# Accumulating over six visits: the running sum of a column tile kept in PSUM by two ScalarE copies instead of one VectorE addition

## The chip, the cores and the metric

The kernel runs on one core of a Trainium2 chip. The metric is device time in microseconds (us), from several executions; the kernel before takes 1729.73 us, the median of three runs between 1729.15 and 1729.89 us. Engines are named as in the profile: PE is TensorE (PEld its weight loads), DVE is VectorE, ACT is ScalarE, SP issues the DMAs.

## What is computed

One layer of a convolutional decoder block on 256 tokens of width 4096, all in float32:

```
mod = silu(c) @ w_ada + b_ada ; shift, scale, gate = split(mod)
h   = rmsnorm(x) * norm_g * (1 + scale) + shift
P   = h @ w_in                      # 4096 x 14336: a_b a_c a_x a_z (mixer A), b_v b_g b_z (mixer B), 2048 columns each
y_A = a_b * conv3(a_c * a_x) * silu(a_z)
y_B = silu(layernorm(conv31(b_v * sigmoid(b_g)) + bias)) * silu(b_z)
x   = x + gate * ([y_A, y_B] @ w_out)
out = rmsnorm(x) * final_g
```

## The kernel before

**Products.** The 4096 rows of the contraction are 32 contraction tiles of 128, the 14336 columns of the input projection are 28 column tiles of 512 (each 2 token tiles x 512 columns, 1024 numbers in each of 128 partitions). A weight load holds two contraction tiles of one column tile (512 KB) and is one step. For each step ScalarE rounds the raw weights `w_r` to `w_h` (L143), VectorE takes the rest `w_l` (L144), and TensorE runs 12 products (L156 to L158: three products for each of two contraction tiles and two token tiles). The weights of the next step are split ahead (`AHEAD = 1`), and there are three buffers for each of `w_h` and `w_l`, so the split of a step can start when the products three steps before it are done. The input projection has 448 steps and the output projection 128.

**Visits.** The activations `hT` of a contraction tile exist only when the conditioning (`mod_steps`, L174, and `make_h`) has reached it. So the contraction is cut into six blocks, and each column tile is visited once per block: 163 visits of 1 to 7 steps (where one block ends with the tile that the next begins with, the two are one visit). The visits in the stretch that is here called the single-step stretch (start of the second block) have one step each; those of the blocks after it have two or three, those of the last block four. Each visit gets a PSUM tile `ps` from the pool `pmm` (three buffers of two banks). At the end of a tile's first visit ScalarE copies `ps` into the SBUF tile `acc[e]` (L467, 28 times); at the end of every other visit VectorE adds `ps` to `acc[e]` (L469, 135 times). These instructions are written right behind the products of the visit.

**Last block.** When a column tile has had its last visit its epilogue follows: tiles 20 to 23 start `glu_B` (a sigmoid, L352, a VectorE product, transposes on TensorE, copies L360 and the first tap L364 on ScalarE) and then 30 taps of the width-31 convolution, spread over the steps (`conv_tap`: four ScalarE products L370 into `pr`, one VectorE addition L371); tiles 12 to 15 start `silu_gate_A` (L324 to L341); tiles 24 to 27 get a silu in place (L480). The taps run on into the output projection. Beside this, the gate columns are worked out from the last block on: the first 2048 on TensorE (L231), whose PSUM tile `gateps` holds one of the three `pmm` buffers meanwhile, the others on VectorE in the output projection.

**Order.** Each engine works through its own queue in a fixed order. `next_w` loads and splits the weights of the next step and then runs the background work that is due at this step (`run_due`); the products of the step follow.

Of the kernel before, what the change touches and what calls it, by code (L numbers as in the profile page):

```python
# [17 lines left out]
P = 128  # L18
D = 4096            # model width
S = 256             # tokens  # L20
NS = S // P         # token tiles
KT = D // P         # contraction tiles
CT = 512            # columns of one product tile
NE = 7 * 2048 // CT  # column tiles of the input projection
NDT = D // CT       # column tiles of the output projection
NB = 16             # channel tiles of mixer B
# [3 lines left out]
BLOCKS = (4, 4, 4, 6, 6, 8)  # contraction tiles done together; the conditioning of a block is  # L30
                             # worked out while the products of the blocks before run
EARLY = {0: 12, 1: 10}  # column tiles, the first of a block, that stop KD contraction tiles short of it
KD = 2              # contraction tiles of one weight load, which is a step
AHEAD = 1           # steps that weights are split ahead
LEAD = 2            # steps from the conditioning of contraction tiles to their first products
KEEP = 3            # chunks of x.T that stay from the row statistics
HOLD = 5            # steps of the last column tile whose weights stay on chip for the second token tile
GATE_PE = (0, 1)    # gate columns (1024 each) worked out on TensorE, the others on VectorE
GATE_RUN = {0: (0, 70), 1: (70, 115), 2: (115, 185), 3: (185, 231)}  # when, in steps from the last block on
A_SPAN = 5          # steps over which the epilogue of 512 channels of mixer A runs  # L40
# steps of the output projection
CONV_END = 43       # when the convolution of mixer B ends
NORM_AT = 45        # when its layernorm starts
NORM_SPAN = 20      # over which it runs
LOAD_AT = 1         # when the residual of a column tile is loaded
TILE_SPAN = 4       # over which a column tile is finished

# columns of the packed small parameters
# [10 lines left out]
def _segments():  # L59
    """[block, column tile, from, to contraction tile] of the input projection, in the order of the products"""  # L60
    order = [16, 20, 17, 21, 18, 22, 19, 23]
    order += [e + i for i in range(4) for e in (4, 8, 0, 12)]
    order += [24, 25, 26, 27]
    segs, done = [], dict.fromkeys(order, 0)
    for b in range(len(BLOCKS)):
        for n, e in enumerate(order if (len(BLOCKS) - 1 - b) % 2 == 0 else order[::-1]):
            k0, k1 = done[e], sum(BLOCKS[:b + 1]) - (KD if n < EARLY.get(b, 0) else 0)
            done[e] = k1
            if n == 0 and b:
                segs[-1][0], segs[-1][3] = b, k1  # L70
            else:
                segs.append([b, e, k0, k1])
    return segs
# [3 lines left out]
FIRST_USE = {}      # contraction tile: the step that needs it first  # L77
for _t, _k in enumerate(k for _, _, k0, k1 in SEGS for k in range(k0, k1, KD)):
    FIRST_USE.setdefault(_k, _t)
UNITS = [[0, KD]]   # contraction tiles conditioned together: the first, their number  # L80
# [8 lines left out]
def decoder_block(ctx: ExitStack, tc: tile.TileContext, x, c, w_mod, w_gate, w_in, w_out, xt, pk, b_gate, final_g, out):  # L89
# [18 lines left out]
    # ---------------- constants and small parameters  # L108
# [17 lines left out]
    def rsqrt(y, v, t):  # L126
        """y = v ** -0.5; v is kept, t is scratch."""
        nc.scalar.activation(out=t, in_=v, func=AF.Sqrt)
        nc.vector.reciprocal(out=y, in_=t)
        nc.vector.tensor_tensor(out=t, in0=y, in1=y, op=ALU.mult)  # L130
        nc.vector.tensor_tensor(out=t, in0=t, in1=v, op=ALU.mult)
        nc.vector.tensor_scalar(out=t, in0=t, scalar1=-0.5, scalar2=1.5, op0=ALU.mult, op1=ALU.add)
        nc.vector.tensor_tensor(out=y, in0=y, in1=t, op=ALU.mult)

    # ---------------- products: out[s, c] += a[k, s] * w[k, c], each operand as two 12-bit parts
# [10 lines left out]

    def products(ps, act, parts, k0, first, last, tokens=range(NS)):
        """act[k // 2][:, k % 2, hi/lo, s] is stationary; ps [P, NS, CT]."""
        hi, lo = parts
        for i in range(KD):  # L150
            a = act[(k0 + i) // 2]
            f, l = first and i == 0, last and i == KD - 1
            for s in tokens:
                out = ps[s] if isinstance(ps, list) else ps[:, s]
                ah, al = (a[:, (k0 + i) % 2, h, s * P:(s + 1) * P] for h in range(2))
                nc.tensor.matmul(out, ah, hi[:, i], start=f, stop=False)  # L156
                nc.tensor.matmul(out, ah, lo[:, i], start=False, stop=False)  # L157
                nc.tensor.matmul(out, al, hi[:, i], start=False, stop=l)  # L158

    def split_act(dst, src):  # L160
        """dst [P, 2, hi/lo, S] <- src [P, 2, S]"""
        nc.scalar.copy(dst[:, :, 0], src)  # L162
        nc.vector.tensor_tensor(out=dst[:, :, 1], in0=src, in1=dst[:, :, 0].bitcast(F32), op=ALU.subtract)

    # ---------------- conditioning: silu(c) @ w_ada, 1024 columns at a time
# [10 lines left out]
    def mod_steps(k0, n):  # L176
        """Shift and scale of contraction tiles k0 .. k0 + n."""
        state = {}

        m = 4 // n      # contraction rows per load  # L180
# [26 lines left out]
    def gate_steps(ci):  # L207
        """Gate of columns 1024 ci .. 1024 ci + 1024, in all partitions."""
# [14 lines left out]
        def step_t(j):  # L223
            # four products with one stationary column each run side by side in the array
            if j == 0:
                state["ps"] = pmm.tile([P, NS, CT], F32, tag="ps", name=f"gateps{ci}")
            raws_ = [load(j), load(j + 1)]
            for i in range(2):
                for h in range(2):
                    r = 32 * (2 * i + h)  # L230
                    nc.tensor.matmul(state["ps"][r:r + 1, 0], cact[:, j + i:j + i + 1], raws_[i][:, h * CT:(h + 1) * CT], start=j == 0, stop=j == KT - 2)  # L231
# [23 lines left out]
    def make_h(k0, n):  # L255
        """h.T = (x * rstd * norm_g * (1 + scale) + shift).T of contraction tiles k0 .. k0 + n, split"""
# [14 lines left out]
    # ---------------- start: row statistics of x, conditioning of the first block  # L271
    kept = []           # x.T of the first contraction tiles

    def x_stats():
        """1 / rms of the rows of x, in all partitions"""
# [28 lines left out]
    # ---------------- background work, spread over the product steps  # L304
    queue = []          # (step at which it is due, closure)
# [9 lines left out]
    # ---------------- mixer epilogues  # L315
    yT = {}

    def silu_gate_A(i, acc):
        """y_A.T of channels [512 i, 512 i + 512), in pieces"""
# [53 lines left out]
    def mean_B(src, name):  # L373
        """mean over the channels: tiles on VectorE, partitions on TensorE"""
# [10 lines left out]
    def norm_B():  # L385
        """layernorm over the channels (partitions), silu, in pieces"""
# [35 lines left out]
    # ---------------- input projection, by blocks of the contraction  # L422
# [8 lines left out]
    def next_w():  # L431
        """the weights of this step; those of the next steps are loaded and split ahead of other work"""
# [7 lines left out]
    # the conditioning runs evenly beside the products  # L440
    hull = [(0, KD)]    # (step, contraction tiles done by then)
# [17 lines left out]
    for b, e, k0, k1 in SEGS:  # L459
        ps = pmm.tile([P, NS, CT], F32, tag="ps", name=f"ps{k0}_{e}")  # L460
        for k in range(k0, k1, KD):
            parts = next_w()
            step += 1
            products(ps, hT, parts, k, k == k0, k + KD == k1)
        if k0 == 0:
            acc[e] = bigt(f"acc{e}")
            nc.scalar.copy(acc[e], ps)  # L467
        else:
            nc.vector.tensor_tensor(out=acc[e], in0=ps, in1=acc[e], op=ALU.add)  # L469
        if k1 < KT:  # L470
            continue
# [6 lines left out]
        elif e >= 24:  # L478
            zB[e - 24] = acc[e]
            nc.scalar.activation(out=acc[e], in_=acc[e], func=AF.Silu)  # L480
        elif 12 <= e < 16:
            work = silu_gate_A(e - 12, acc)
            spread(work, step, step + A_SPAN)

    # ---------------- output projection: the channels of mixer A, then those of mixer B
# [5 lines left out]
    for dt in range(NDT):  # L491
        ps = pmm.tile([P, NS, CT], F32, tag="ps", name=f"pa{dt}")
        for k in range(0, KT // 2, KD):
            parts = next_w()
            step += 1
            products(ps, yT, parts, k, k == 0, k + KD == KT // 2)
# [3 lines left out]
    # gate, residual, final norm  # L500
# [4 lines left out]
    def finish_tile(dt, ps):  # L505
        """gate, residual, sums of squares and final weight of a column tile, in pieces"""
# [60 lines left out]
    # the last column tile: the first token tile's products, then the second's while the first is finished  # L567
# [28 lines left out]
def _columns(a):  # L596
    """[n * 128, ...] -> [128, n, ...], flat per partition"""
# [35 lines left out]
```

## Time and profile before

| | |
|---|---|
| median of three runs | 1729.73 us |
| span of the profiled execution | 1728.9 us |
| what lies around the span, against the median | 0.8 us |
| PE busy | 1669.5 us, 97% |
| DVE busy | 1506.9 us, 87% |
| ACT busy | 937.0 us, 54% |
| DMA | 302 GB/s in the mean |

The table's shares are means over the whole span; the work differs by stage. The input projection's second block begins near 177 us, its last block runs from about 984 to 1354 us, and the output projection follows. A PE that is 97% busy has its matmuls overlapping one another (each lasts some 390 ns and the next starts after 227 ns), so its delays are seen better in the distance between steps than in its busy share: twelve products at full pace take 2.72 us.

### The profile page before, as it was taken

The page shows a single profiled execution, that of the slowest core. Times are in us where ns is not written, and L with a number is a line of the kernel's source. Part 1 is how long each engine was busy: PE and PEld are TensorE (multiplying, and loading weights), DVE is VectorE, ACT ScalarE, POOL GpSimd, SP SyncE. Part 2 cuts the span into 40 slices and gives each one's busy share as a digit, 9 for nine tenths or more (in the row PEclk, how much of TensorE's full clock was granted, in tenths as well). Part 3 has the DMA queues.
Part 4 walks back from the last instruction along what each step waited for, and adds up shares of the span by engine and source line. Part 5 has one row for each costly group of instructions (what it writes and reads, how often), then busy time and mean ns, then how long its engine had stood idle before and what let it go on. Part 6 is the DMA issues. An engine that isn't in the chain of part 4 may idle for free.

```text
span 1728.9 us, 21319 instructions
## 1 busy us (share of the span) xinstructions
PE 1669.5 (97%) x7480; PEld 1340.1 (78%) x7480; DVE 1506.9 (87%) x1490; ACT 937.0 (54%) x1304; POOL 2.9 (0%) x10
## 2 busy tenths in 40 slices
PE   2899999999999999999999999999999999999997
PEld 1778788888888888888888877777777887878885
DVE  7887998899898988898898857898998999989996
ACT  3555443443334333343333468888887888564443
POOL 0000000000000000000000000000000000000000
PEclk8899999999999999999999999999999999999998
DMA  9899899999999998999899977766888888779993
GB/s 387 327 317 331 300 344 327 325 320 332 310 335 326 330 326 302 312 352 329 292 340 321 327 243 248 253 230 232 288 278 281 277 286 280 266 254 335 361 345 116
DMA packets 145715, 522.42 MB, mean 302 GB/s; under 512 B 16196, under 2 KB 16196, under 8 KB 145608
## 3 DMA queue, kind: packets, MB, share of 16 engines
q1 hardware_dynamic: 145464, 520.71, 85.8%
q8 instruction: 58, 0.95, 0.2%
q10 hardware_dynamic: 144, 0.35, 0.1%
q14 instruction: 49, 0.40, 0.1%
HBM read 516.81 MB, written 4.19 MB: 301 GB/s over the span
## 4 chain that ended last, share of the span: by engine, by line
PE 86%; DVE 6%; DMA 4%; issue 3%; ACT 1%; SPq 0%; DVEq 0%; ACTq 0%
PE ps L156 23%; PE ps L157 23%; PE ps L158 23%; PE pb L158 3%; PE pb L156 3%; PE pb L157 3%; DVE w_l L144 2%; PE gateps L231 2%; DMA gate<-in_w_gate 2%; DVE cv L371 1%; PE pa L157 1%; PE pa L158 1%; DVE modacc L174 1%; PE pa L156 1%; DMA mod<-in_w_mod 1%
## 5 line engine op out<-in xcount | busy, mean ns | idle before, releaser
L143 ACT CAST w_h<-w_r 128x1024 fp32r<-128x1024 f32 x576 | 603.7, 1052 | 654.2 <-PE ps L158 490.4
L144 DVE TENSOR_TENSOR w_l<-w_r,w_h 128x1024 fp32r<-128x1024 f32 x576 | 700.8, 1220 | 118.8 <-ACT w_h L143 113.2
L156 PE MATMUL ps<-w_h,hT 128*128 128x512 f32 x1792 | 705.8, 394 | 3.0 <-ACT hT L162 2.6
L157 PE MATMUL ps<-w_l,hT 128*128 128x512 f32 x1792 | 700.7, 391 | 5.6 <-DVE w_l L144 5.6
L158 PE MATMUL ps<-w_h,hT 128*128 128x512 f32 x1792 | 699.4, 390 | 0.0
L156 PEld LDWEIGHTS ps<-w_h,hT 128*128 128x128 f32 x1792 | 337.5, 188 | 96.8 <-issue 10.8
L157 PEld LDWEIGHTS ps<-w_l,hT 128*128 128x128 f32 x1792 | 337.5, 188 | 79.9 <-DVE w_l L144 10.9
L158 PEld LDWEIGHTS ps<-w_h,hT 128*128 128x128 f32 x1792 | 337.3, 188 | 70.6
L174 DVE SCALAR_TENSOR_TENSOR modacc<-mod,cact,modacc 128x512 f32<-128x512 f32 (+1 forms) x341 | 337.4, 990 | 4.6 <-DMA mod<-in_w_mod 1.5
L370 ACT ACTIVATE pr<-uT,pks 128x255 f32<-128x255 f32 (+14 forms) x480 | 198.1, 487 | 2.1 <-DVE cv L371 1.6
L469 DVE TENSOR_TENSOR acc<-ps,acc 128x1024 f32<-128x1024 f32 x135 | 164.9, 1221 | 22.9 <-PE ps L158 22.4
L371 DVE TENSOR_TENSOR cv<-cv,pr 128x1020 f32<-128x1020 f32 (+14 forms) x120 | 138.7, 1156 | 27.1 <-ACT pr L370 26.4
L157 PE MATMUL pa<-w_l,yT 128*128 128x512 f32 x256 | 100.6, 393 | 2.4 <-DVE w_l L144 2.4
L156 PE MATMUL pa<-w_h,yT 128*128 128x512 f32 x256 | 100.1, 391 | 0.0
L156 PE MATMUL pb<-w_h,yT 128*128 128x512 f32 x256 | 100.1, 391 | 0.0
L158 PE MATMUL pb<-w_h,yT 128*128 128x512 f32 x256 | 100.0, 391 | 0.0
L158 PE MATMUL pa<-w_h,yT 128*128 128x512 f32 x256 | 100.0, 390 | 0.0
L157 PE MATMUL pb<-w_l,yT 128*128 128x512 f32 x256 | 99.6, 389 | 0.0
L174 DVE SCALAR_TENSOR_TENSOR gateacc<-gate,cact,gateacc 128x1024 f32<-128x1024 f32 x62 | 79.4, 1280 | 5.8 <-DMA gate<-in_w_gate 5.6
L157 PEld LDWEIGHTS pa<-w_l,yT 128*128 128x128 f32 x256 | 48.0, 188 | 14.6 <-DVE w_l L144 4.8
L467 ACT COPY acc<-ps 128x1024 f32<-128x1024 f32 x28 | 28.5, 1017 | 51.7 <-PE ps L158 51.7
L156 PEld LDWEIGHTS pb<-w_h,yT 128*128 128x128 f32 x256 | 48.1, 188 | 10.3 <-ACT w_h L143 0.2
(129 smaller groups left out, 645.2 us busy)
## 6 DMA issues: line engine op xcount, KB each, us to landing
w_r<-in_w_in SPq DMA_DIRECT2D x448, 512.0 KB, 5.2
mod<-in_w_mod SPq DMA_DIRECT2D x256, 512.0 KB, 5.1
gate<-in_w_gate SPq DMA_DIRECT2D x128, 512.0 KB, 4.8
w_r<-in_w_out SPq DMA_DIRECT2D x128, 512.0 KB, 5.1
xs<-in_xt SPq DMA_DIRECT2D x8, 512.0 KB, 10.2
xr<-in_x SPq DMA_DIRECT2D x8, 512.0 KB, 7.0
out<-o SPq DMA_DIRECT2D x16, 256.0 KB, 2.7
xc<-in_xt SPq DMA_DIRECT2D x4, 512.0 KB, 5.2
```

Of the source, the lines that this page charges most:

```text
L143: nc.scalar.copy(hi, raw)
L144: nc.vector.tensor_tensor(out=lo, in0=raw, in1=hi.bitcast(F32), op=ALU.subtract)
L156: nc.tensor.matmul(out, ah, hi[:, i], start=f, stop=False)
L157: nc.tensor.matmul(out, ah, lo[:, i], start=False, stop=False)
L158: nc.tensor.matmul(out, al, hi[:, i], start=False, stop=l)
L174: nc.vector.scalar_tensor_tensor(out=acc, in0=raw, scalar=cact[:, j:j + 1], in1=acc, op0=ALU.mult, op1=ALU.add)
L231: nc.tensor.matmul(state["ps"][r:r + 1, 0], cact[:, j + i:j + i + 1], raws_[i][:, h * CT:(h + 1) * CT], start=j == 0, stop=j == KT - 2)
L370: nc.scalar.activation(out=pr[:, j, sh:], in_=u[:, j, :S - sh], func=AF.Copy, scale=cbw[:, 4 * i + j, TAPS - 1 - sh:TAPS - sh])
L371: nc.vector.tensor_tensor(out=o[:, :, sh:], in0=o[:, :, sh:], in1=pr[:, :, sh:], op=ALU.add)
L467: nc.scalar.copy(acc[e], ps)
L469: nc.vector.tensor_tensor(out=acc[e], in0=ps, in1=acc[e], op=ALU.add)
```

## The change

The sum of a column tile is now held in PSUM during a visit. Ahead of a visit that is not the tile's first, ScalarE copies `acc[e]` into the visit's `ps` (`seed`), written at the last step of the visit before; the products of the visit then add to it (`start` is set only where the contraction starts at tile 0). At the end ScalarE copies `ps` back to `acc[e]` (`take`), and for the last visit of tiles 24 to 27 this copy is the silu itself, in place of the silu on `acc[e]`. `take`, with the epilogue that it starts, is written one step later than before: in the first step of the next visit, behind that step's weight split and background work. There is no VectorE addition. Elsewhere only comments and docstrings went.

```
-    def products(ps, act, parts, k0, first, last, tokens=range(NS)):
+    def products(ps, act, parts, k0, first, last, tokens=range(NS), seeded=False):
...
-                nc.tensor.matmul(out, ah, hi[:, i], start=f, stop=False)
+                nc.tensor.matmul(out, ah, hi[:, i], start=f, stop=False, skip_group_check=seeded)
...
-    for b, e, k0, k1 in SEGS:
+    pending = []
+    def seed(n):
+        _, e, k0, _ = SEGS[n]
         ps = pmm.tile([P, NS, CT], F32, tag="ps", name=f"ps{k0}_{e}")
-        for k in range(k0, k1, KD):
-            parts = next_w()
-            step += 1
-            products(ps, hT, parts, k, k == k0, k + KD == k1)
-        if k0 == 0:
+        if k0:
+            nc.scalar.copy(ps, acc[e])
+        return ps
+    def take(e, k1, ps):
+        nonlocal conv_start
+        if e not in acc:
             acc[e] = bigt(f"acc{e}")
-            nc.scalar.copy(acc[e], ps)
-        else:
-            nc.vector.tensor_tensor(out=acc[e], in0=ps, in1=acc[e], op=ALU.add)
+        nc.scalar.activation(out=acc[e], in_=ps, func=AF.Silu if k1 == KT and e >= 24 else AF.Copy)
         if k1 < KT:
-            continue
+            return
         if 20 <= e < 24:
...
         elif e >= 24:
             zB[e - 24] = acc[e]
-            nc.scalar.activation(out=acc[e], in_=acc[e], func=AF.Silu)
         elif 12 <= e < 16:
...
+    ps = seed(0)
+    for n, (b, e, k0, k1) in enumerate(SEGS):
+        for k in range(k0, k1, KD):
+            parts = next_w()
+            step += 1
+            while pending:
+                pending.pop()()
+            if k + KD == k1 and n + 1 < len(SEGS):
+                ps_next = seed(n + 1)
+            products(ps, hT, parts, k, k == 0, k + KD == k1, seeded=k0 > 0)
+        pending.append(lambda e=e, k1=k1, ps=ps: take(e, k1, ps))
+        ps = ps_next
...
+            while pending:          # in the first half of the output projection
+                pending.pop()()
             products(ps, yT, parts, k, k == 0, k + KD == KT // 2)
```

## Rows read from the trace of the kernel before

**Rows 1.** The page: busy time, share of the span and instructions of each engine.
```profile
PE 1669.5 (97%) x7480; PEld 1340.1 (78%) x7480; DVE 1506.9 (87%) x1490; ACT 937.0 (54%) x1304; POOL 2.9 (0%) x10
```
**Rows 2.** The page: busy tenths in 40 slices of 43 us.
```profile
PE   2899999999999999999999999999999999999997
...
DVE  7887998899898988898898857898998999989996
ACT  3555443443334333343333468888887888564443
```
**Rows 3.** The page: the chain that ended last, by engine.
```profile
PE 86%; DVE 6%; DMA 4%; issue 3%; ACT 1%; SPq 0%; DVEq 0%; ACTq 0%
```
**Rows 4.** Waits of PE, 80 to 1560 us (us in total, times, longest).
```profile
PE ps L157 <- DVE w_l L144: 5.6, 10, 1.4
PE pa L157 <- DVE w_l L144: 2.4, 4, 1.0
```
**Rows 5.** Waits of PE, single-step stretch, 190 to 213 us.
```profile
PE ps L157 <- DVE w_l L144: 2.0, 5, 0.6
```
**Rows 6.** Busy time by stretch (us, PE, PEld, DVE, ACT, POOL, PE clock, DMA).
```profile
190.40:213.00 22.60, 20.56 (x86) 15.37 (x85) 22.60 (x26) 7.34 (x7) 0.00 (x0) 1.00 0.81 264
225.60:236.50 10.90, 10.90 (x50) 9.03 (x49) 10.87 (x10) 4.22 (x4) 0.00 (x0) 1.00 1.00 355
1018.20:1236.20 218.00, 218.00 (x1021) 160.89 (x1020) 183.86 (x179) 188.38 (x350) 0.95 (x1) 1.00 0.73 244
1236.20:1353.80 117.60, 117.60 (x566) 85.34 (x565) 101.25 (x107) 93.01 (x171) 0.00 (x0) 1.00 0.83 282
```
**Rows 7.** Groups of VectorE instructions, 190.4 to 213.0 us (busy, mean ns, idle before).
```profile
L174 DVE SCALAR_TENSOR_TENSOR modacc<-mod,cact,modacc 128x512 f32<-128x512 f32 x12 | 8.9, 743 | 0.0
L469 DVE TENSOR_TENSOR acc<-ps,acc 128x1024 f32<-128x1024 f32 x7 | 8.5, 1218 | 0.0
L144 DVE TENSOR_TENSOR w_l<-w_r,w_h 128x1024 fp32r<-128x1024 f32 x7 | 8.5, 1217 | 0.0
```
**Rows 8.** Groups of the whole span.
```profile
L469 DVE TENSOR_TENSOR acc<-ps,acc 128x1024 f32<-128x1024 f32 x135 | 164.9, 1221 | 22.9 <-PE ps L158 22.4
L467 ACT COPY acc<-ps 128x1024 f32<-128x1024 f32 x28 | 28.5, 1017 | 51.7 <-PE ps L158 51.7
L480 ACT ACTIVATE acc<-acc 128x1024 f32<-128x1024 f32 x4 | 4.2, 1056 | 0.0
```
**Rows 9.** Timeline of ACT, 1004 to 1060 us (start us, us, instruction, idle before).
```profile
1006.34 1.05 ACT L143 CAST w_h<-w_r 128x1024 fp32r<-128x1024 f32 x1 [1.67 <-PE ps L158]
1009.06 1.05 ACT L143 CAST w_h<-w_r 128x1024 fp32r<-128x1024 f32 x1 [1.67 <-PE ps L158]
...
1024.07 1.07 ACT L360 COPY uT<-psU 128x512 f32<-128x512 f32 x2 [1.28 <-PE psU L359]
1025.03 2.08 ACT L364 ACTIVATE cv<-uT,pks 128x256 f32<-128x256 f32 x4
1027.01 1.70 ACT L370 ACTIVATE pr<-uT,pks 128x255 f32<-128x255 f32 x4
1028.61 2.00 ACT L143 CAST w_h<-w_r 128x1024 fp32r<-128x1024 f32 x2
```
**Rows 10.** VectorE additions of 17 visits, 1018.2 to 1236.2 us.
```profile
L469 DVE TENSOR_TENSOR acc<-ps,acc 128x1024 f32<-128x1024 f32 x17 | 20.8, 1222 | 4.4 <-PE ps L158 4.3
```
**Rows 11.** Waits of ACT, 1018.2 to 1236.2 us.
```profile
ACT w_h L143 <- PE ps L158: 14.8, 17, 1.7
ACT yT L162 <- DVE yfA L341: 5.0, 3, 2.8
...
ACT uT L360 <- PE psU L359: 2.2, 3, 1.3
ACT yfA L338 <- PE psA L336: 1.7, 1, 1.7
ACT pr L370 <- DVE cv L371: 1.6, 4, 0.8
```
**Rows 12.** VectorE additions of 9 visits, 1236.2 to 1353.8 us.
```profile
L469 DVE TENSOR_TENSOR acc<-ps,acc 128x1024 f32<-128x1024 f32 x9 | 11.0, 1221 | 1.4 <-PE ps L158 1.4
```

More of the change, by code (lines that the diff above doesn't have):

```diff
@@ L155, in products @@
                 ah, al = (a[:, (k0 + i) % 2, h, s * P:(s + 1) * P] for h in range(2))
-                nc.tensor.matmul(out, ah, hi[:, i], start=f, stop=False)
-                nc.tensor.matmul(out, ah, lo[:, i], start=False, stop=False)
-                nc.tensor.matmul(out, al, hi[:, i], start=False, stop=l)
+                nc.tensor.matmul(out, ah, hi[:, i], start=f, stop=False, skip_group_check=seeded)
+                nc.tensor.matmul(out, ah, lo[:, i], start=False, stop=False, skip_group_check=seeded)
+                nc.tensor.matmul(out, al, hi[:, i], start=False, stop=l, skip_group_check=seeded)
     def split_act(dst, src):
```

## Prediction

> **What bounds the kernel now.** I read the page's busy shares first: TensorE 97%, VectorE 87%, ScalarE 54% [rows 1]. The chain that ended last agrees: 86% of it is PE, 6% VectorE, 1% ScalarE [rows 3]. So the change takes work from an engine that is second in line and gives it to one that looks idle; what that is worth depends on where PE really waits for VectorE. The waits of PE say: from 80 to 1560 us only 5.6 us in ten waits for `w_l` in the input projection, and 2.4 us in four in the output projection, where nothing was added into `acc` anyway [rows 4]. The 164.9 us of additions [rows 8] are therefore almost all hidden. Then I read the slices, because a mean over stages hides the stage: ScalarE is at 3 to 4 tenths through most of the input projection, but at 8 tenths in the slices of the last block, where the convolution's taps run on it [rows 2]. These two places, the single-step stretch and the last block, decide the sum.
>
> **VectorE's additions go (a gain).** There are 135 of 1.221 us [rows 8]. The only stretch in which they lie on the path is the one of single-step visits: from 190.4 to 213.0 us VectorE is busy 22.60 of 22.60 us [rows 6], with 7 additions (8.5 us) beside 7 weight splits (8.5 us) and 12 conditioning rows (8.9 us) [rows 7], and PE waits there for `w_l` [rows 5]. Seven steps ran in these 22.6 us. A step at full pace is 2.72 us, the distance of two `w_h` that each wait for PE to free a buffer [rows 9], so 7 x 2.72 = 19.0 us and 3.6 us were lost. (The waits show only 2.0 us of it, since a matmul lasts longer than the distance to the next one.) Without the additions VectorE has 17.0 us of work for 19.0 us, and the loss goes. What is late next there is ScalarE: a single-step visit now costs it a split (1.05 us), a take and a seed. A copy of this size out of PSUM is 1.017 us [rows 8]; two copies in a row last 1.07 us where one of them alone is some 0.59, and two splits 2.00 us against 2 x 1.05 [rows 9], so neighbours overlap by some 0.10 us. Back to back a take is 0.92 us. No row has ScalarE writing PSUM. The nearest rows bound the seed: 1.017 us (out of PSUM) and 1.056 us (SBUF to SBUF) [rows 8], that is 0.92 to 0.96 back to back; I take 0.94, the middle. A pair is 1.86 us. With the split (0.95 back to back) this is 2.81 us per step against 2.72, over nine such visits 0.8 us behind. ScalarE may be late by about 5.44 - 1.05 - 1.22 = 3.2 us before PE notices: a split can start two steps ahead of its products, less its own time and that of `w_l`. So the cover nearly holds; I take a gain of 3.0 us, between 2.8 and 3.6.
>
> **The other visits up to the last block (nothing).** Two-step visits give ScalarE 5.44 us, of which it works 4.22 of 10.9 [rows 6], about 2.1; with a pair 4.0. Three-step visits leave more. Cover: the products themselves. If the cover were gone, a seed would stand between two visits and cost up to 1.0 us each. The additions removed here hid behind PE already. The copies of the 28 first visits stay, one step later. DMA issues do not change in number; SP waits for buffers that VectorE frees, and VectorE is earlier.
>
> **The last block (a loss).** From 1018.2 to 1236.2 us there are 17 additions [rows 10], so 17 visits end. ScalarE is busy 188.4 of 218.0 us [rows 6]: 29.6 us idle, or 1.74 us per visit. A pair costs 1.86, so 17 x 1.86 = 31.6 us: 2.0 us too much even with no idle time left. Part of the idle time can't be filled with certainty. 14.8 us of it is `w_h` waiting for PE to free a buffer; that is ScalarE's lead, and a pair fits in. But 10.5 us are waits on VectorE or PE in the middle of an epilogue: 5.0 for `yfA`, 2.2 for `psU`, 1.7 for `psA`, 1.6 for `cv` [rows 11]. The 5.0 I let go, as VectorE loses 20.8 of its 183.9 us there; the other 5.5 stay. Against this stands the lead of 3.2 us, which can be spent once. So 2.0 + 5.5 - 3.2 = 4.3 us of delay. Bounds: 0 (all waits filled, the lead pays the 2.0) and 17 x 2.07 - 29.6 + 10.5 = 16.1 us (no overlap, 1.017 + 1.056 per pair, no wait filled, no lead).
>
> After that, 1236.2 to 1353.8 us: ScalarE idles 117.6 - 93.0 = 24.6 us [rows 6]; nine pairs [rows 12] are 16.7 us and three silus of about 0.95 us, now part of a take, come off. It fits: nothing.
>
> **What the later take moves.** Take, sigmoid and convolution start one step later and behind that step's split and taps. A take waits for the visit's last product; behind it on ScalarE stand the next `w_h`, taps, and the seed. In a four-step visit the seed comes three steps after that take, so the wait costs lead, not path. PSUM: while `gateps` holds a buffer two are left, and the seed of the visit after next needs the take to be done, again three steps earlier. In the output projection only the last take arrives, with nothing behind it that is due. Nothing for these; each would cost about one copy, 1 us, per visit if the order is worse than I think.
>
> The sum against the profiled execution: 1728.9 - 3.0 + 4.3 = 1730.2 us; the median of the runs is 0.8 us above that span, so **1731.0 us**.
>
> **A rule of the skill weighed against the rows.** The rows above show a copy out of PSUM 0.04 us shorter than an activation between SBUF tiles [rows 8]. The Trainium skill's page "ScalarE: Activation LUTs", section "What ACT_TABLE_LOAD costs", gives an activation with immediate scale and bias 186 ns + 0.833 ns per element, and an overlap of some 93 ns back to back: an estimate of 1.04 us here, 0.95 back to back, so a pair of 1.89 us and a last block later by 17 x 0.03 = 0.5 us. The same page, in the step-by-step section, says that ScalarE writes PSUM faster than SBUF, by which the seed would be nearer to my lower end; no row here shows it. The sum stays on the rows.
>
> **Rivals.**
> (a) *Only the gain.* The list of instructions on ScalarE is such that pairs fill the lead and the epilogue's waits shrink because VectorE is earlier: 1729.7 - 3.6 = 1726.1, and with up to 1 us of the 2.4 us in the output projection [rows 4] 1725. For it: 14.8 us of pure lead [rows 11]. Against it: idle time of 1.74 per visit is under the price of a pair, before any wait. 20%.
> (b) *ScalarE becomes the bound of the last block.* The mechanism is the queue between 1018 and 1236 us: each pair over 1.74 us makes all later splits late, and PE waits for `w_l` and for the seed. At 2.07 per pair with no wait filled, 16.1 - 3.2 = 12.9 us, less 2.8: 1729.7 + 10.1 = 1739.8 us. It decides the sign from about 3 us of delay on, more than the gain pays. For it: ScalarE at 8 to 9 tenths there [rows 2] and the 4.5 us chunk of copies, first taps and products between two splits at 1024 us, where `w_h` had no turn [rows 9]. Against it: the idle stretch after 1236 us lets it catch up. 30%.
> On (b) the Trainium skill's same page, section "Rules for kernel authors", says to do plain adds and multiplies on VectorE, not on ScalarE; here one addition of 1.22 us becomes two copies of 2.03 to 2.07.
> (c) *The seed does not run ahead.* If the fixed order puts seeds behind work that waits for PE, each boundary pays the copy: about 1 us in each of the 26 visits of the last block, +26 - 3: about 1753 us. For it: takes that wait for PE stand ahead of seeds in the same queue. Against: three steps of distance in these visits. 5%.
>
> **How the numbers follow.** The measurement can tell 0.2%, 3.5 us, from no change: below 1726.3 is faster, above 1733.2 slower. The forecast (a small gain against a small loss) 45%, its own range 1727 to 1734. It lies within 0.2% for the most part. (a) 20% is faster; (b) and (c) 35% slower. So faster 0.20, same 0.45, slower 0.35. The range reaches from the end of (a) to the end of (b): 1725 to 1740; (c) is left out with the tail of (a).
>
> **What would show it.** Right: in the single-step stretch steps of 2.72 us with no wait of PE for VectorE; VectorE's busy time down by some 165 us; ScalarE's up by 135 x 1.86 less the silus, about 250 us; a ScalarE busy over 95% of 1018 to 1236 us, and new waits of PE there, a few us in all, on `w_h`, on `w_l` behind it, or on the seed. Wrong: no such waits (then (a)), waits of PE of over 8 us there ((b)), a wait on the seed at most boundaries ((c)), or a single-step stretch that stays slow because ScalarE or the conditioning takes VectorE's place. A seed shorter than 0.8 us or longer than 1.2 us would upset the price of the pair.

## The result: slower by 0.67%, just outside the range

The changed kernel takes 1741.55 us in the median of four runs (1740.45 to 1742.11) against 1729.81 us before; the ratio is 1.0067, interval 1.0053 to 1.0081. The forecast was 1731.0 us, the range 1725 to 1740. The profiled execution has a span of 1740.2 us, 11.3 more than before.

The page after: busy time of each engine.
```profile
PE 1676.8 (96%) x7480; PEld 1339.1 (77%) x7480; DVE 1363.7 (78%) x1355; ACT 1168.1 (67%) x1570; POOL 2.9 (0%) x10
```
Against [rows 1] VectorE lost 143 us and ScalarE gained 231 (the prediction had 165 and 250); the work moved as it was meant to. The groups of the two copies after, over the whole span:
```profile
L475 ACT ACTIVATE acc<-ps 128x1024 f32<-128x1024 f32 x163 | 167.3, 1027 | 219.1 <-PE ps L158 218.8
L467 ACT COPY ps<-acc 128x1024 f32<-128x1024 f32 x135 | 137.1, 1016 | 0.3
```
A seed is 1.016 us, at the lower end of the bounds, and ScalarE idles 0.3 us in all ahead of the seeds; a take is 1.027 us, and ScalarE idles 219 us ahead of the takes, waiting for the visit's products.

Where the time went is read from the start of each stage's first product, by counting twelve products a step in both traces. The step numbers are those of the plan; 344 to 447 is the stretch from 1018.2 to 1353.8 us before, the first 68 steps of the output projection follow it.

| us | before | after | difference |
|---|---|---|---|
| up to step 42 (start and first block) | 176.8 | 175.5 | -1.3 |
| 42 to 103 (single-step stretch and next visits) | 175.8 | 173.2 | -2.6 |
| 104 to 343 | 665.7 | 665.8 | 0.1 |
| 344 to 447 (last block from the first taps on) | 335.6 | 346.7 | 11.1 |
| 448 to 515 (output projection, first part) | 197.0 | 200.9 | 3.9 |
| 516 to the last product | 165.6 | 165.6 | 0.0 |

The first line is no effect: in the traces of the kernels below the first 42 steps take anything from 123.4 to 126.1 us, with the additions as with the copies. The other three differences are effects; the last of them is the least certain, since the stretch 448 to 515 differs by about 1 us between traces of kernels that do the same there (below). The early gain is there: busy time by stretch (us, PE, PEld, DVE, ACT, POOL, PE clock, DMA), the rows after that answer to [rows 6]. The first covers the same seven steps as there, the third the same 68.
```profile
189.10:210.40 21.30, 20.66 (x94) 16.41 (x92) 16.75 (x22) 20.75 (x23) 0.00 (x0) 1.00 0.92 320
225.60:236.50 10.90, 10.90 (x50) 9.01 (x49) 8.33 (x8) 7.87 (x9) 0.00 (x0) 1.00 0.86 303
1014.50:1242.10 227.60, 225.89 (x1023) 160.90 (x1021) 165.36 (x160) 212.93 (x376) 0.96 (x1) 1.00 0.69 235
1014.50:1361.20 346.70, 344.99 (x1585) 246.26 (x1584) 258.27 (x258) 319.33 (x564) 0.96 (x1) 1.00 0.72 248
```
In the single-step stretch VectorE went from 22.6 of 22.6 us to 16.75 of 21.3, and ScalarE is now the busy one, 20.75 of 21.3. PE's waits there after, 188 to 213 us, against [rows 5]:
```profile
PE ps L157 <- DVE w_l L144: 0.8, 3, 0.4
```
The loss there is smaller, but not gone. Steps 47 to 55 took 29.7 us before and 27.2 after; nine steps at full pace are 24.5. Of the 2.7 us that stay, 0.9 are the conditioning's products on TensorE, and most of the rest is `w_l` coming late behind `w_h`. ScalarE's queue shows why: a take stands ahead of the next split and waits for PE, although that split's buffer had been free since the products of step 44 ended at 183.8 us (rows of ACT and PE after).
```profile
186.58 1.03 ACT L475 ACTIVATE acc<-ps 128x1024 f32<-128x1024 f32 x1 [0.64 <-PE ps L158]
187.50 1.04 ACT L143 CAST w_h<-w_r 128x1024 fp32r<-128x1024 f32 x1
...
189.85 0.50 PE L157 MATMUL ps<-w_l,hT 128*128 128x512 f32 x1 [0.37 <-DVE w_l L144]
```
In the last block ScalarE is busy 319 of 347 us, 92%: loaded, but not full. And PE's waits there are few. First PE's waits after from 1014.5 to 1361.2 us:
```profile
PE ps L156 <- ACT w_h L143: 0.6, 1, 0.6
PE ps L156 <- ACT ps L467: 0.6, 1, 0.6
PE ps L157 <- DVE w_l L144: 0.4, 1, 0.4
```
These 1.6 us of waiting do not make 11.1 us. The rest is found by asking what PE does with the time. Groups of PE in the last block: the gate products before (1018.2 to 1353.8 us) and, in the second fence, after.
```profile
L231 PE MATMUL gateps<-gate,cact 128*1 128x512 f32 x232 | 33.2, 591 | 0.0
```
```profile
L231 PE MATMUL gateps<-gate,cact 128*1 128x512 f32 x232 | 40.3, 591 | 0.0
```
The same 232 records, the same 591 ns each, but 7.1 us more busy time. Four gate products form a group (eight records, two per product): they write four different PSUM partitions (0, 32, 64, 96) and run side by side, so that eight records of 591 ns are over in 1.04 us. TensorE's timeline shows what happened to the groups. Before, a group stands whole between two steps:
```profile
1104.47 0.39 PE L158 MATMUL ps<-w_h,hT 128*128 128x512 f32 x1
1104.79 1.04 PE L231 MATMUL gateps<-gate,cact 128*1 128x512 f32 x8
1105.76 0.50 PE L156 MATMUL ps<-w_h,hT 128*128 128x512 f32 x1
```
After, many are broken. Here two records stand between the first and the second product of a step, and the other six four steps later.
```profile
1087.29 1.02 PE L231 MATMUL gateps<-gate,cact 128*1 128x512 f32 x2
1088.24 0.50 PE L157 MATMUL ps<-w_l,hT 128*128 128x512 f32 x1
...
1102.95 1.03 PE L231 MATMUL gateps<-gate,cact 128*1 128x512 f32 x6
1103.91 0.50 PE L156 MATMUL ps<-w_h,hT 128*128 128x512 f32 x1
```
Two records take 1.02 us, six 1.03, eight 1.04: a piece costs what a whole group costs. Counted over both traces, 10 of the 32 groups are broken after and 3 before.

### The profile page after: what moved, and what is told of

It reads as the page before. It is cut to its first block, busy times and chain, and to the rows that moved or that the text cites. A ratio compares the mean times of both kernels' runs of the same rounds, so it can differ in the third digit from the quotient of the medians.

```text
span 1740.2 us, 21489 instructions
## 1 busy us (share of the span) xinstructions
PE 1676.8 (96%) x7480; PEld 1339.1 (77%) x7480; DVE 1363.7 (78%) x1355; ACT 1168.1 (67%) x1570; POOL 2.9 (0%) x10
## 4 chain that ended last, share of the span: by engine, by line
PE 85%; DVE 6%; DMA 4%; issue 3%; ACT 2%; SPq 0%; DVEq 0%; ACTq 0%
PE ps L156 23%; PE ps L157 23%; PE ps L158 23%; PE pb L156 3%; PE pb L158 3%; PE pb L157 3%; PE gateps L231 2%; DVE w_l L144 2%; DMA gate<-in_w_gate 2%; DVE cv L371 1%; PE pa L157 1%; PE pa L158 1%; PE pa L156 1%; PE modps L197 1%; ACT w_h L143 1%
## 5 line engine op out<-in xcount | busy, mean ns | idle before, releaser
L174 DVE SCALAR_TENSOR_TENSOR modacc<-mod,cact,modacc 128x512 f32<-128x512 f32 (+1 forms) x341 | 337.5, 990 | 4.8 <-DMA mod<-in_w_mod 1.5
L475 ACT ACTIVATE acc<-ps 128x1024 f32<-128x1024 f32 x163 | 167.3, 1027 | 219.1 <-PE ps L158 218.8
L467 ACT COPY ps<-acc 128x1024 f32<-128x1024 f32 x135 | 137.1, 1016 | 0.3
L156 PEld LDWEIGHTS pa<-w_h,yT 128*128 128x128 f32 x256 | 48.1, 188 | 10.3 <-ACT w_h L143 0.2
```

Source lines behind the costliest of these rows:

```text
L156: nc.tensor.matmul(out, ah, hi[:, i], start=f, stop=False, skip_group_check=seeded)
L174: nc.vector.scalar_tensor_tensor(out=acc, in0=raw, scalar=cact[:, j:j + 1], in1=acc, op0=ALU.mult, op1=ALU.add)
L467: nc.scalar.copy(ps, acc[e])
L475: nc.scalar.activation(out=acc[e], in_=ps, func=AF.Silu if k1 == KT and e >= 24 else AF.Copy)
```

## Experiments

Two theories were set up for the last block. S: broken groups, an order on TensorE that came out differently, each 1.05 us. B: ScalarE is late, and the pieces only fill time in which PE would wait. Later O, for the output projection: `w_l` stands behind gate rows on VectorE. Each kernel ran beside the kernel before on the same chip. Edits are shown shortened. Stretches are given as in the table (the early stretch is steps 42 to 103, the last block 344 to 447, the output projection 448 to 515), each from one trace. Where an expectation gives some 347 or 344 us for a whole last block of a kernel with whole groups, it counts from step 340, which adds 12 us to 335 and 332. The 208.3 us that one expectation gives for the output projection run to step 519.

**Whole gate groups in the changed kernel.**
```
-  nc.tensor.matmul(gate product i, h)
+  if i or h:
+      with tc.high_priority():
+          nc.tensor.matmul(gate product i, h)
+  else: nc.tensor.matmul(gate product i, h)
```


> Changed kernel, with one edit: of the four gate products of a group on TensorE (L231) the second to fourth get a high priority, so each of the 32 groups stands unbroken in TensorE's queue; in the changed kernel 10 of 32 stand broken as 1 + 3, in the kernel before 3. Theory S (broken groups): each broken group costs 1.05 us more, since the four products of a group run side by side and a group of one, three or four lasts about 1.05 us alike; 10 x 1.05 = 10.5 us off the last block: 346.7 -> about 336 to 338 us, the whole near 1731 us. Theory B (ScalarE is late): TensorE's time was only filled with pieces while it would have waited anyway; the pieces come back as waits on w_h, w_l and the seed, last block 345 us or more, the whole 1740 us.

1731.28 us; ratio to before 1.0005 (0.9996 to 1.0015). The last block is 335.1 us, 11.6 less than after, or 1.16 us for each of ten groups. S holds: time that the pieces would only have filled would have come back as waits, but PE's waits there are the same 1.6 us. The output projection stays at 201.0.

**VectorE adds again in the last block.**
```
-        if k0: nc.scalar.copy(ps, acc[e])
+        if k0 and b < 5: nc.scalar.copy(ps, acc[e])     # else the visit starts fresh and is added by VectorE
```


> Changed kernel, but the visits of the last block are added on VectorE as before (silu in place again); the seeds and takes of all earlier visits stay. Both theories: the loss of the last block goes (346.7 -> 336 us) and the gain of the single-step stretch and the start (3.9 us) stays: 1726 us if the output projection also returns to 208.3 us, 1730 us if its 3.9 us stay. If the loss had come from the earlier visits' copies it would stay at 1740.

1731.89 us; ratio 1.0011 (1.0001 to 1.0021). Last block 337.5 us, early stretch 173.2, output projection 198.7. The time is 1.9 us above the higher of the two that were expected. Most of the loss is gone, though the last block is 1.9 us over the old one: the take, now a VectorE addition again, still comes one step later, and 4 groups are broken, one more than before. So it is the copies of the last block that break the other groups; the next run is the counterpart.

**Only the last block seeded** (the counterpart of the same condition, `b == 5`).

> The counterpart: VectorE adds in all visits except those of the last block, which are seeded and taken by ScalarE. Both theories: the last block's loss without the gain, 1729.8 + 11.1 + 3.9 = 1744.8 us, the same ten broken groups; S expects 346 to 347 us for the last block again. If the early visits were part of the last block's loss, less.

1744.02 us; ratio 1.0081 (1.0066 to 1.0096). Last block 346.7 us, gate products 40.3 us busy and ten broken groups as in the changed kernel; early stretch 175.9, output projection 199.9. The two effects add: early copies win 2.6 us, late ones lose the rest.

**The price of a piece: the kernel before with groups halved.**
```
-            raws_ = [load(j), load(j + 1)]
-            for i in range(2): for h in range(2): matmul(...)
+            raw = load(j)
+            for h in range(2): matmul(...)          # one closure per j
```


> Kernel before, with each group of four gate products written as two groups of two, half as far apart; nothing else. The price of a broken group by itself. Theory S: a group lasts about 1.05 us whatever its size, so 32 groups more cost 32 x 1.05 = 34 us: 1763 us. Theory B: a piece costs in proportion to its products, so nothing: 1730 us.

1764.67 us; ratio 1.02 (1.0185 to 1.0215). The expectation counts 32 pieces more, but the kernel before has 35 already, three groups being broken: 64 pieces are 29 more, and 34.6 us are 1.19 us each. Half a group, four records, in this kernel's timeline of PE:
```profile
1108.45 1.03 PE L229 MATMUL gateps<-gate,cact 128*1 128x512 f32 x4
```
S's price stands by itself, with no copy involved. It is somewhat over the 1.03 us of the row: 1.16 to 1.19 us here and in the runs with whole groups.

**Whole groups in the kernel before** (the edit of the first experiment).

> Kernel before with the gate groups kept whole by the same priority; nothing else. Theory S (broken groups): the kernel before has 3 broken groups at 1.05 us: last block 347.6 -> 344.5 us, the whole 1726.9 us. It is also the fair base for the copies' own cost: in the changed kernel with whole groups the last block took 347.1 us, so ScalarE's added work would cost 2.6 us there. Theory B (the groups cost nothing): 1730 us.

1727.08 us; ratio 0.998 (0.9971 to 0.9989): faster, by 3.5 us for three groups. Last block 332.1 us. Against it the changed kernel with whole groups needs 335.1, 3.0 us more. This is all that is left of the loss of the last block. Not all of it is the copies': with additions on VectorE there, a step late, and whole groups the kernels of the last three experiments need 332.9. So 0.8 us come with the later take and 2.2 with the copies. PE does not wait there at all in this kernel, and 1.6 us in the changed one with whole groups.

**`w_l` first in the output projection, changed kernel with whole groups.**
```
+        if len(loaded) >= end_in:
+            with tc.high_priority():
                 nc.vector.tensor_tensor(out=lo, ...)
```


> Changed kernel with whole gate groups, and in the output projection the splits w_l on VectorE get a high priority, so that they stand ahead of gate rows (L174) and taps in VectorE's queue. Theory O (order on VectorE): the 4 us that the output projection lost (197.0 -> 200.9 and 201.0 us from its first to its 68th step) are w_l standing behind gate rows that wait for their DMA; they go: 195 to 197 us there, the whole 1725 to 1727 us. Rival (ScalarE or the DMAs are late there): 201 us stay, the whole 1731 us.

1727.98 us; ratio 0.9985 (0.9976 to 0.9994). Output projection 198.2 us, not 195 to 197. PE's waits in it, the changed kernel with whole groups first (1350.7 to 1551.7 us), then this one (1348.7 to 1547 us):
```profile
PE pa L157 <- DVE w_l L144: 4.8, 5, 1.9
```
```profile
PE pa L161 <- DVE w_l L146: 2.6, 4, 1.4
PE psZ L426 <- DVE cv L427: 1.7, 1, 1.7
```
O explains 2.8 of the 4.0 us; the wait for `w_l` falls, and part of it turns into one for the layernorm's tail, which the priority pushes back. VectorE's own waits fit: in the changed kernel, 1361.2 to 1562.1 us,
```profile
DVE gateacc L174 <- DMA gate<-in_w_gate: 9.2, 7, 2.5
```
VectorE, which works its queue in order, waits 9.2 us for gate rows to land, with the splits behind (5.6 us in the kernel before). The whole time agrees: the intervals of this kernel and of the changed kernel with whole groups (0.9996 to 1.0015) do not meet. Why the order there came out worse than before is not settled.

**A third copy: ScalarE's limit.**
```
+        if k1 == KT: nc.scalar.copy(acc[e], ps)
         nc.scalar.activation(out=acc[e], in_=ps, ...)
```


> Changed kernel with whole gate groups and a third copy on ScalarE for each of the 28 last visits: the take is done twice, first as a plain copy. The output is the same. 26 x 0.92 = 24 us more work for ScalarE in the last block, 319 + 24 = 343 of 347 us. If ScalarE's load is what costs time there (theory B), the block grows by most of it: 347.1 -> 360 us or more, the whole 1745 us. If the load still hides in ScalarE's idle time (theory S): at most 5 us more, with about 2 us for two groups that stand broken as 2 + 2: the whole under 1737 us.

1738.93 us; ratio 1.0049 (1.0034 to 1.0065). Last block 344.8 us, 9.7 more than with two copies: between the two expectations. Busy time of the last block, this kernel, and PE's waits in it:
```profile
1013.80:1358.60 344.80, 338.38 (x1586) 246.76 (x1585) 256.37 (x256) 338.78 (x587) 0.95 (x1) 1.00 0.71 248
```
```profile
PE ps L156 <- ACT ps L472: 4.0, 4, 1.5
PE ps L157 <- DVE w_l L144: 1.2, 3, 0.5
PE gateps L236 <- DMA gate<-in_w_gate: 1.2, 1, 1.2
```
With ScalarE at 338.8 of 344.8 us, 98%, PE waits 4.0 us for seeds (and some 2.3 us of the 9.7 are the two groups that are broken here). So theory B's mechanism exists, one copy per visit further on than the change went.

**Putting it together: copies only before the last block, whole groups, `w_l` first.**

> Seeds and takes only in the visits before the last block, VectorE additions in the last block, whole gate groups, w_l first in the output projection: what the theories S and O together recommend. Gain of the early visits 2.6 us, of the three whole groups 3.2 us, of the output projection 1 to 4 us: 1720 to 1724 us. If only run-to-run differences were at work in the output projection: 1724 us.

1725.67 us; ratio 0.9974 (0.9963 to 0.9984). The lowest median of this study, though above the 1720 to 1724 expected, and not clear of the kernel before with whole groups alone (0.998, 0.9971 to 0.9989). Last block 332.9, early stretch 173.2, output projection 197.5 us.

**The same, copies only in single-step visits.**

> As early_only (whole gate groups, w_l first in the output projection), but seeds and takes only in the single-step visits of the second block; VectorE adds in all other visits. If the early gain of 2.6 us comes from the single-step stretch alone, as the prediction had it: 1725.7 us like early_only, 173.2 us from step 42 to 103. If the two- and three-step visits had a part in it: 175 us there and 1728 us.

1726.21 us; ratio 0.9976 (0.9966 to 0.9986). The early stretch is 174.0 us: 1.8 of the 2.6 us come from the copies of the single-step visits, 0.8 from those of the visits after them. The output projection, where this kernel does what the last one does, is 198.6 us against 197.5: a difference of 1.1 us between two traces with no difference in the source there. The totals of the two can't be told apart.

**Copies before the last block and whole groups, without the priority for `w_l`.**

> As early_only, but without the priority for w_l in the output projection. Theory O says what the priority itself is worth where the last block is VectorE's again: 198.7 us from step 448 to 515 (as in lastadd) against 197.5 in early_only, 1727 us in all. If the order on VectorE is not it: 1725.7 us.

1727.39 us; ratio 0.9983 (0.9974 to 0.9992). Output projection 198.7 us, against 197.5 and 198.6 in the two kernels with the priority. Here O is not shown: the difference is no larger than that between those two, and the intervals of the totals overlap. Against the kernel before with whole groups alone (0.998) the early copies bring nothing that can be measured in the whole: their 2.6 us stand against 0.8 more in the last block and 0.8 more in the output projection (198.7 against 197.9).

## Why the prediction was wrong, point by point

- *VectorE's additions go, a gain of 3.0 us in the single-step stretch*: right in sign, but mis-sized. Steps 42 to 103 gained 2.6 us, under the range of 2.8 to 3.6, and only 1.8 of it comes from the copies of the single-step visits. PE waits there 0.8 us for `w_l` instead of 2.0 [rows 5]. ScalarE is what is late next, as said, but the cover of 3.2 us does not hold: the reckoning had splits free to run ahead, while in ScalarE's queue takes that wait for PE stand in front of them (the rows at 186.58 us).
- *The other visits up to the last block, nothing*: right for steps 104 to 343 (0.1 us); the two- and three-step visits before them gained 0.8 us. In two-step visits ScalarE works 7.87 of 10.9 us, 3.9 us per visit where the prediction had 4.0.
- *The price of a pair, 1.86 us*: right where the copies are apart, with a split behind each (0.92 us from a take to the split, 0.94 from a seed, medians from 350 to 1000 us after). In the single-step stretch a seed follows a take directly, without the overlap of 0.10 us that was reckoned with, and a step costs ScalarE 2.96 us, not 2.81 (rows below). A seed by itself is 1.016 us against the bounds 1.017 to 1.056. The Trainium skill remarks ("ScalarE: Activation LUTs", step-by-step section) that ScalarE writes PSUM faster than SBUF; the rows agree as far as they go: the seed (SBUF to PSUM) takes 1.016 us, a split `w_h` (SBUF to SBUF, of the same size) 1.048. The estimate of 1.04 us from that page was a little high for both copies.
```profile
195.49 1.05 ACT L143 CAST w_h<-w_r 128x1024 fp32r<-128x1024 f32 x1
196.44 1.03 ACT L475 ACTIVATE acc<-ps 128x1024 f32<-128x1024 f32 x1
197.49 1.02 ACT L467 COPY ps<-acc 128x1024 f32<-128x1024 f32 x1
198.45 1.05 ACT L143 CAST w_h<-w_r 128x1024 fp32r<-128x1024 f32 x1
```
- *The last block, a loss of 4.3 us*: this is the step that failed. The block lost 11.1 us. What the sum worked out there, ScalarE's lateness under the copies, measured 2.2 us, and 0.8 us more came with the later take, which the prediction had put at nothing. The other 8.1 us were nowhere in the sum: seven more broken gate groups on TensorE, shown three ways (made whole, halved without any copy, and gone or back with the last block's copies). Rival (b) names the right place and nearly the right total, but by luck: its mechanism, the queue on ScalarE, would have shown as waits of PE of over 8 us, and there were 1.6. The prediction counted the instructions that the change adds and removes on each engine and took the order of all others as given, without a reason. It is not given: the gate products on TensorE, which the change does not touch, came to stand elsewhere.
- *The later take, nothing; the output projection, nothing*: besides the 0.8 us above, the output projection lost 3.9 us. VectorE's queue there has gate rows ahead of splits in other places, and with whole groups 2.8 us go when the splits are put first (one trace each, with about 1 us between traces). The rest is open.
- *ScalarE busy over 95% from 1018 to 1236 us, with waits on the seed*: 212.9 of 227.6 us, 94%, in the same steps, and one wait of 0.6 us on a seed.
- (a) and (c) did not happen: the kernel is not faster, and one seed in the last block was waited for.

That the copies break the groups is shown. Why they do is open. One idea is that `w_l` is ready later in the reckoning by which the queues are ordered, so that a gate product is put into the gap between a step's first product (which needs `w_h`) and the first that needs `w_l`. In the trace after, six of the ten broken groups have a piece in such a gap; the other four have both pieces between steps or beside transposes, so the idea is at most a part of it.

## What to carry to other kernels

When a change loads an engine that feeds the bound, look at what the bound's own queue looks like afterwards, not only at its waits: here TensorE was as busy as before (96% against 97%) and did the same products, in an order that cost 1.16 to 1.19 us per broken group. Work that is cheap only because it stands together (the gate products that run side by side) should be kept together explicitly; doing that alone made the kernel before 0.2% faster. And a relief belongs where the relieved engine is full: the copies won 1.8 us in the nine single-step visits, where VectorE was at 100%, 0.8 us in the visits behind them and nothing from there on, and in the whole time even this gain could not be told from none.

## What the runs showed of the hardware

One, two, three or four gate products with a single stationary column, written to PSUM partitions 0, 32, 64 and 96, take 1.02 to 1.04 us alike, so four in a group cost 0.26 us each and one alone four times that. Between ordinary products such a piece cost 1.16 to 1.19 us. ScalarE carried 95% of a stretch (318.7 of 335.1 us with whole groups) while PE waited 1.6 us; at 98% the stretch was 9.7 us longer, some 2.3 of it for two broken groups.
